# Memory cross-attention in a decoder trunk: the two heads of a group taken through one chain, with other delays behind the copies

## The chip, the core and the metric

One core of one Trainium2 chip runs the whole program. The metric is device microseconds from start to end of one execution, the median of several. Engines: PE (TensorE, matrix products), ACT (ScalarE), DVE (VectorE), POOL (GpSimd), SP (SyncE, which issues the transfers here). The times before are 1011.96, 1012.36 and 1012.1 us: median 1012.1 us.

## What is computed

A decoder trunk of two layers on 256 tokens of width 1024, all in fp32. Each layer is a SwiGLU feed-forward block at half weight, a mixing block, and a second feed-forward block. The mixing block of layer 0 has 4 mLSTM heads, that of layer 1 has 16 sliding-window heads (window 128, 2 key heads, partial rotary embedding, a learned sink per head). In both, 4 memory cross-attention heads of size 128 over 256 memory rows stand beside them, fed by the same input projection and the same output projection:

```python
proj = hn @ a_w_in[j]                     # layer 1: b_w_in[j]
y_tok = mlstm_heads(proj[..., :A_TOK], ...)   # layer 1: swa_heads(...)
y_mem = memory_heads(proj[..., A_TOK:], mem_k, mem_v, xa_q_norm_g[i], xa_k_norm_g[i])
x = x + jnp.concatenate([y_tok, y_mem], axis=-1) @ w_out

def memory_heads(xq, mem_k, mem_v, q_norm_g, k_norm_g):
    q = rms_norm(xq.reshape(bsz, t, M_HEADS, M_HD), q_norm_g)
    k = rms_norm(mem_k, k_norm_g)
    s = jnp.einsum('bthd,bmhd->bhtm', q, k) * M_HD ** -0.5
    p = jax.nn.softmax(s, axis=-1)
    return jnp.einsum('bhtm,bmhd->bthd', p, mem_v).reshape(bsz, t, M_Q)
```

## The kernel before

**Numbers and tiles.** Activations lie transposed, width on partitions, as tiles `[128, 2, 256]` (512 columns). For the projections every fp32 value is split into a high and a low part, and each tile product is three matmuls (`mm3`, lines 225, 226 and 227). A weight tile comes by a transfer into `wr` (5 buffers), ACT casts its high part into `wh` (line 211, 128x1024), DVE subtracts for the low part `wl` (line 212); 8 buffers each. Attention uses plain fp32 products: `mmf` (line 231; one instruction in the code is two or more passes on PE) and `transpose` (line 236). All results of PE go into one pool of 8 PSUM banks of `[128, 512]` fp32; `mo()` takes the next, and a bank comes free when its last reader is done.

**Who sets the order.** PE's and SP's order is that of the program text, and the text is interleaved by the class `Weave`. A main chain (projections, in pieces of 12 matmuls) runs; chains that were spawned beside it, each a Python generator, are stepped between its pieces once they are due. Due times are in a modelled clock, `wv.now`, which each product advances by a fixed cost; `yield d` means "not before d later", and the delays stand in one dictionary, `LAT` (lines 53 to 55). So `LAT` decides how many projection matmuls stand on PE between, say, a transposition and the product that reads its copy. ACT, DVE and POOL take their instructions in an order that a scheduler writes for each at build time; each engine then runs its own list strictly in order.

**Cross-attention, `cross_spawn`** (lines 568 to 611), for a group of two heads. `head_norm` (368 to 385) normalises the queries: a Square on ACT, a reduce on DVE (374), two small operations (377), a power on POOL (379), two small ones (381), and the multiplication (383), which is also the last reader of the group's projection bank. The chain `queries` transposes them (`turn`, 387) and copies them with a scale (`qT`, the ACT operation with `gqk`; all calls of the helper `act` show line 132). It spawns one chain `head(m)` for each of the two heads, `cross_s` later and `cross_m` between them. A head: two products into one bank (scores), a reduce for the maxima (591), two Exps on ACT with sums, a reciprocal (595), a multiplication (596); `cross_p` later four transpositions into one bank and a copy (603); `cross_o` later the values, two products into half of a bank, and `split_plain` of 256 columns (copy on ACT, line 245; subtraction on DVE, line 246). Then the head's rows of the output projection may be used (`ys.done`).

**Layer 1, `mixer_b`** (863 to 974). The main chain projects keys and values, the two cross query groups, and four query groups of four window heads each. Each query group goes through `head_norm`, rotary operations (857 to 860), `turn` and a scaled copy (`qr`, with `gcut`), and then two chains `head(ch)` (910 to 965), each for two window heads in two banks: a mask product into each bank (920), scores (925), reduces for maxima (929, 930), minima with the sinks (932, 933), four Exps and one for the sinks, sum and reciprocal (941, 942), four scalings (946); `head_p` later transpositions into two banks with two copies (954); `head_o` later values (961) and `split_plain`. Then the output projection: `out_proj` takes rows 8 to 11 (the cross heads) first, then 0 to 5, and last 6 and 7; `ys.has` steps other chains until a row's head is done. Layer 0, `mixer_a` (649 to 804), uses the same `cross_spawn` beside its mLSTM chains.

Of the kernel before, what the change touches and what calls it, by code (L numbers as in the profile page):

```python
# [10 lines left out]
F32 = mybir.dt.float32  # L11
# [3 lines left out]
AF = mybir.ActivationFunctionType  # L15
ALU = mybir.AluOpType
AX = mybir.AxisListType
PSUM = bass.MemoryType.PSUM

P = 128  # L20
T = 256
# [11 lines left out]
def constants():  # L33
# [16 lines left out]

LAT = dict(pieces=1, norm=7.5, norm_b=4.8, mnorm=2.4, x0=16.0, x0_b=7.5, mkeys=7.2, cross=9.5, cross_s=1.5,
           cross_m=3.7, cross_p=8.7, cross_o=3.0, gates=20.0, scores=2.2, scores_m=8.4, num=6.9, num_r=7.5,
           keys=5.5, keys_d=7.2, query=9.0, head=1.5, head_m=2.5, head_p=9.3, head_o=4.0)


WARM = 18
# [40 lines left out]
def tile_trunk(ctx: ExitStack, tc: tile.TileContext, a, out):  # L99
    nc = tc.nc  # L100
    seq = [0]

    def mk(pool, shape, dt, tag):
        seq[0] += 1
        return pool.tile(shape, dt, tag=tag, name=f"{tag}_{seq[0]}")
# [5 lines left out]
    wv = Weave()  # L111
# [16 lines left out]
    tt = nc.vector.tensor_tensor  # L128
    tabled = [None]

    def act(*args, **kw):
        ins = nc.scalar.activation(*args, **kw)  # L132
        if args[2] not in (AF.Copy, AF.Square):
            tabled[0] = ins
# [6 lines left out]
    def unit(dt):  # L141
        return mk(up, [P, 2, T], dt, "u")

    def tmp():
        return mk(tp, [P, 2, T], F32, "t")

    def col():
        return mk(cp, [P, 16], F32, "col")

    def mo():  # L150
        return mk(pb8, [P, 512], F32, "bank")

    def halves(ps):
        return ps.rearrange("p (h t) -> p h t", h=2)
# [48 lines left out]
    pieces = [1]  # L203
# [26 lines left out]
    def mmf(ps, lhsT, rhs, n, start=True, stop=True):  # L230
        nc.tensor.matmul(ps, lhsT, rhs, start=start, stop=stop, skip_group_check=True)  # L231
        wv.now += max(0.213, n * 0.00182)

    def transpose(ps, src):
        k = src.shape[0]
        nc.tensor.transpose(ps, src, ident[:k, :k])  # L236
        wv.now += 0.107
# [6 lines left out]
    def split_plain(src, hi, lo):  # L244
        nc.scalar.copy(hi, src)
        tt(out=lo, in0=src, in1=hi.bitcast(F32), op=ALU.subtract)
# [14 lines left out]
    class Norm:  # L261
# [30 lines left out]

        def chain(self, gap=LAT['norm_b']):
            pc = mo()
            for h in range(2):
                mmf(pc[:, h:h + 1], self.acc[:, 0, h * P:(h + 1) * P], ones, 1)
            self.rc = mk(sp, [P, 2], F32, "rc")
            rsqrt_cols(self.rc, pc[:, 0:2], 2, 1.0 / D)
            if not self.rows:
                self.done = True  # L300
                return
            yield gap
            ps = mo()
            bcast_rows(ps, self.rc)
            self.rb = mk(sp, [P, T], F32, "rb")
            nc.scalar.copy(self.rb, ps[:, :T])
            if self.half:
                self.hrb = mk(sp, [P, T], F32, "hrb")
                act(self.hrb, ps[:, :T], AF.Copy, scale=0.5)
            self.done = True  # L310
# [57 lines left out]
    def head_norm(dst, src, n, hsc):  # L368

        hd = src.shape[2] // n  # L370
        sq, v, u = tmp(), col(), col()
        sqv = sq[:, :, :n * hd]
        act(sqv, src, AF.Square)
        nc.vector.tensor_reduce(out=v[:, 0:2 * n].rearrange("p (h m) -> p h m", h=2),
                                in_=sqv.rearrange("p h (m d) -> p h m d", m=n), axis=AX.X, op=ALU.add)
        for h in range(2):
            nc.vector.tensor_scalar(u[:, n * h:n * h + n], v[:, n * h:n * h + n], hsc[:, h:h + 1], EPS,
                                    op0=ALU.mult, op1=ALU.add)
        nc.gpsimd.tensor_tensor(out=u[:, 8:8 + 2 * n], in0=u[:, 0:2 * n], in1=mhalf[:, 0:2 * n], op=ALU.pow)  # L379
        for h in range(2):  # L380
            nc.vector.tensor_scalar(v[:, 8 + n * h:8 + n * h + n], u[:, 8 + n * h:8 + n * h + n],
                                    hsc[:, 2 + h:3 + h], None, op0=ALU.mult)
        tt(out=dst.rearrange("p h (m d) -> p h m d", m=n), in0=src.rearrange("p h (m d) -> p h m d", m=n),  # L383
           in1=v[:, 8:8 + 2 * n].rearrange("p (h m) -> p h m", h=2).unsqueeze(3).to_broadcast([P, 2, n, hd]),
           op=ALU.mult)

    def turn(rows):

        ps = mo()
        for m in range(2):  # L390
            for h in range(2):
                transpose(ps[:, m * T + h * P:m * T + (h + 1) * P], rows[:, h, m * P:(m + 1) * P])
        return halves(ps)


    kT = [mk(cst, [P, 2, T], F32, f"kT{i}") for i in range(2)]
    vM = mk(cst, [P, 2, 512], F32, "vM")
    x0 = Norm(G_F1)

    def memory():  # L400
# [22 lines left out]
        def keys(gi, kr):  # L423
            nc.scalar.copy(kT[gi], turn(kr))
            return
            yield

        for gi in range(2):
# [13 lines left out]
            norm.fold()  # L442
            wv.spawn(norm.chain(), LAT['mnorm'])
            gv = Group(wkv, 512, mh, ml, rows=True)
# [5 lines left out]
            for i, q in enumerate((first, gr)):  # L450
                kr = tmp()
                head_norm(kr, q.ps, 2, hsc)
                wv.spawn(keys(i, kr), LAT['mkeys'] + 1.5 * i)
        for gi in range(2):
# [7 lines left out]
            if gi == 0:  # L462
                with tc.issue_after(last[0].ins):
                    for c2 in range(4):
                        x0.put(xT[c2])
                wv.spawn(x0.chain(LAT['x0_b']), LAT['x0'])

# [41 lines left out]
    def ffn(x, w_in, w_out, nxt=None, mid=None):  # L509
# [13 lines left out]
        for c2 in range(4):  # L523
# [25 lines left out]
            else:  # L549
                nxt.put(xn)  # L550
        wv.spawn(nxt.chain(), LAT['norm'])

# [15 lines left out]
    def cross_spawn(gr, gi, layer, hsc, ys):  # L568
        qn = unit(F32)
        head_norm(qn, gr.ps, 2, hsc)  # L570
        cell = []

        def queries():
            ps = turn(qn)
            qT = unit(F32)
            act(qT, ps, AF.Copy, scale=gqk[:, layer:layer + 1])
            cell.append(qT)
            for m in range(2):
                wv.spawn(head(m), LAT['cross_s'] + LAT['cross_m'] * m)
            return  # L580
            yield

        def head(m):
            hd, qT = gi * 2 + m, cell[0]
            hi, lo = ys.tiles(4 + gi)
            s = mo()
            for h in range(2):
                mmf(s[:, h * T:(h + 1) * T], qT[:, m, h * P:(h + 1) * P], kT[gi][:, m], T)
            sv = halves(s)
            c = col()  # L590
            nc.vector.tensor_reduce(out=c[:, 2:4], in_=sv, axis=AX.X, op=ALU.max, negate=True)  # L591
            p = unit(F32)
            for h in range(2):
                act(p[:, h], sv[:, h], AF.Exp, bias=c[:, 2 + h:3 + h], accum_out=c[:, 4 + h:5 + h])
            nc.vector.reciprocal(c[:, 6:8], c[:, 4:6])
            tt(out=p, in0=p, in1=c[:, 6:8].unsqueeze(2).to_broadcast([P, 2, T]), op=ALU.mult)
            yield LAT['cross_p']
            tps = mo()
            for mc in range(2):
                for h in range(2):  # L600
                    transpose(tps[:, mc * T + h * P:mc * T + (h + 1) * P], p[:, h, mc * P:(mc + 1) * P])
            pT = tmp()
            nc.scalar.copy(pT, halves(tps))
            yield LAT['cross_o']
            o = mo()
            for mc in range(2):
                mmf(o[:, :T], vM[:, mc, hd * P:(hd + 1) * P], pT[:, mc], T, mc == 0, mc == 1)
            split_plain(o[:, :T], hi[:, m], lo[:, m])
            ys.done.add(8 + hd)

        wv.spawn(queries(), LAT['cross'])


# [413 lines left out]
```

## Time and profile before

| | |
|---|---|
| runs | 1011.96, 1012.36, 1012.1 us |
| profiled execution | 1012.23 us, of which 1010.4 us is the span from its first to its last instruction |
| granted clock of PE | 1.00 of full speed |
| mixer_a | about 225 to 356 us of the span |
| mixer_b | about 718 to 845 us of the span |

How to read it: the profile shows one execution. A row of the timeline gives start, duration, engine, line, operation, output and inputs, and, in brackets, how long the engine was idle before it and what released it; "x4" are four instructions in a row of one shape. L12 is line 12 of the kernel. The view of waits adds up such idle times by what ended them, the view by windows gives busy times in a stretch, and the groups by line give busy us, mean ns of one and the idle time ahead. The rest of the span, outside the two mixers, is feed-forward work.

### The profile page before, as it was taken

To read this page: it belongs to the slowest core of one execution; us is meant where nothing else is said; L and a number is where in the kernel's file an instruction comes from. 1 tells how busy PE (TensorE), PEld (TensorE's weight loads), DVE (VectorE), ACT (ScalarE), POOL (GpSimd) and SP (SyncE) were. 2 spreads that over 40 slices of the span, in tenths; PEclk is the share of its full clock that TensorE was granted. 3 is DMA by queue.
4 is the path that set the end of the run, shared out by engine and by line. 5 is a ranking of instruction groups with operands and counts; after the bars stand their busy time and mean duration, and the time that the engine had idled before them with its cause. 6 is when DMAs were issued, how large, how long until landed. Compare 5 with 4: busy or idle time off the path is not lost.

```text
span 1010.4 us, 20624 instructions
## 1 busy us (share of the span) xinstructions
PE 998.5 (99%) x8594; PEld 980.2 (97%) x8594; DVE 655.5 (65%) x1063; ACT 519.5 (51%) x764; POOL 35.7 (4%) x32
## 2 busy tenths in 40 slices
PE   8999999999999999999999999999999999999998
PEld 7999999999999999999999999999987899999998
DVE  6866665577856676665558666656787766666551
ACT  7754445446656554444445544544557754454440
POOL 1200000000001000000000000000121000000000
PEclk9999999999999999999999999999999999999999
DMA  9776656666644566665676666567541347666550
GB/s 308 242 245 200 192 180 185 199 183 179 184 139 133 167 210 195 200 189 170 192 206 205 189 191 201 173 197 198 182 131 66 100 131 220 198 189 185 188 170 21
DMA packets 173204, 182.70 MB, mean 181 GB/s; under 512 B 7124, under 2 KB 168328, under 8 KB 173112
## 3 DMA queue, kind: packets, MB, share of 16 engines
q1 hardware_dynamic: 171872, 179.60, 58.3%
q10 hardware_dynamic: 1016, 1.58, 0.5%
q8 instruction: 67, 1.10, 0.5%
q0 software_dynamic: 224, 0.22, 0.2%
q14 instruction: 25, 0.20, 0.1%
HBM read 180.32 MB, written 1.05 MB: 180 GB/s over the span
## 4 chain that ended last, share of the span: by engine, by line
PE 94%; DVE 3%; ACT 1%; DMA 1%; POOL 0%; issue 0%; SPq 0%; ACTq 0%
PE bank L225 30%; PE bank L226 30%; PE bank L227 30%; PE bank L231 2%; PE bank L236 1%; ACT u L132 1%; DVE wl L212 1%; DMA wr<-in_mem_w_kv_dram 1%; PE bank L961 1%; POOL col L379 0%; DVE col L930 0%; DVE u L383 0%; DVE col L591 0%; PE bank L925 0%; DVE u L946 0%
## 5 line engine op out<-in xcount | busy, mean ns | idle before, releaser
L212 DVE TENSOR_TENSOR wl<-wr,wh 128x1024 fp32r<-128x1024 f32 (+1 forms) x347 | 414.7, 1196 | 279.8 <-ACT wh L211 279.0
L211 ACT CAST wh<-wr 128x1024 fp32r<-128x1024 f32 (+1 forms) x347 | 356.8, 1031 | 393.1 <-PE bank L226 368.9
L225 PE MATMUL bank<-xh,wh 128*128 128x256 f32 x1544 | 429.1, 278 | 0.0
L226 PE MATMUL bank<-xl,wh 128*128 128x256 f32 x1544 | 426.8, 276 | 0.0
L227 PE MATMUL bank<-xh,wl 128*128 128x256 f32 x1544 | 426.8, 276 | 0.0
L226 PEld LDWEIGHTS bank<-xl,wh 128*128 128x128 f32 x1544 | 290.3, 188 | 0.1
L225 PEld LDWEIGHTS bank<-xh,wh 128*128 128x128 f32 x1544 | 290.0, 188 | 0.1
L227 PEld LDWEIGHTS bank<-xh,wl 128*128 128x128 f32 x1544 | 289.9, 188 | 0.0
L225 PE MATMUL bank<-u,wh 128*128 128x256 f32 x896 | 249.3, 278 | 0.0
L226 PE MATMUL bank<-u,wh 128*128 128x256 f32 x896 | 247.6, 276 | 0.0
L227 PE MATMUL bank<-u,wl 128*128 128x256 f32 x896 | 247.6, 276 | 0.0
L225 PEld LDWEIGHTS bank<-u,wh 128*128 128x128 f32 x896 | 168.2, 188 | 1.9 <-issue 1.7
L226 PEld LDWEIGHTS bank<-u,wh 128*128 128x128 f32 x896 | 168.4, 188 | 0.1
L227 PEld LDWEIGHTS bank<-u,wl 128*128 128x128 f32 x896 | 168.3, 188 | 0.0
L225 PE MATMUL bank<-wh,xh 128*128 128x256 f32 x208 | 59.7, 287 | 0.0
L226 PE MATMUL bank<-wl,xh 128*128 128x256 f32 x208 | 57.9, 278 | 0.0
L227 PE MATMUL bank<-wh,xl 128*128 128x256 f32 x208 | 57.9, 278 | 0.0
L476 DVE TENSOR_TENSOR t<-bank,rb 128x256 f32<-128x256 f32 x88 | 36.6, 420 | 7.3 <-PE bank L227 7.3
L225 PEld LDWEIGHTS bank<-wh,xh 128*128 128x128 f32 x208 | 39.1, 188 | 0.5 <-issue 0.3
L226 PEld LDWEIGHTS bank<-wl,xh 128*128 128x128 f32 x208 | 39.1, 188 | 0.1
L227 PEld LDWEIGHTS bank<-wh,xl 128*128 128x128 f32 x208 | 39.0, 187 | 0.0
L479 DVE TENSOR_TENSOR t<-t,bank 128x256 f32<-128x256 f32 x88 | 32.7, 412 | 1.8 <-ACT t L132 1.8
(171 smaller groups left out, 657.5 us busy)
## 6 DMA issues: line engine op xcount, KB each, us to landing
wr<-in_ffn_w_in_dram SPq DMA_DIRECT2D x176, 512.0 KB, 3.6
wr<-in_ffn_w_out_dram SPq DMA_DIRECT2D x80, 512.0 KB, 3.5
wr<-in_a_w_in_dram SPq DMA_DIRECT2D x28, 512.0 KB, 3.9
wr<-in_b_w_in_dram SPq DMA_DIRECT2D x14, 512.0 KB, 4.6
wr<-in_a_w_out_dram SPq DMA_DIRECT2D x12, 512.0 KB, 3.3
wr<-in_b_w_out_dram SPq DMA_DIRECT2D x12, 512.0 KB, 3.4
wr<-in_ffn_w_out_dram SPq DMA_DIRECT2D x16, 256.0 KB, 2.8
wr<-in_mem_w_kv_dram SPq DMA_DIRECT2D x7, 512.0 KB, 8.0
```

What stands on the lines that cost most here:

```text
L132: ins = nc.scalar.activation(*args, **kw)
L211: last[0] = nc.scalar.copy(hi[:, i * n:(i + 1) * n], src[:, i * n:(i + 1) * n])
L212: tt(out=lo[:, i * n:(i + 1) * n], in0=src[:, i * n:(i + 1) * n], in1=hi[:, i * n:(i + 1) * n].bitcast(F32), op=ALU.subtract)
L225: nc.tensor.matmul(ps, wh, xh, start=start, stop=False, skip_group_check=True)
L226: nc.tensor.matmul(ps, wh, xl, start=False, stop=False, skip_group_check=True)
L227: nc.tensor.matmul(ps, wl, xh, start=False, stop=stop, skip_group_check=True)
L231: nc.tensor.matmul(ps, lhsT, rhs, start=start, stop=stop, skip_group_check=True)
L236: nc.tensor.transpose(ps, src, ident[:k, :k])
L476: tt(out=t[:, m], in0=ps[m][:, :T], in1=x.rb, op=ALU.mult)
L479: tt(out=t[:, m], in0=t[:, m], in1=ps[m][:, T:], op=ALU.mult)
L961: nc.tensor.matmul(o[es[e], cs], vr[:, i, js], pTs[e][:, src], start=i == 0, stop=i == 1, skip_group_check=True)
```

## The change

Both heads of a cross group now go through one chain, `heads()`: two score banks and four products in a row, the softmax of the one and the other, one pause `cross_p`, eight transpositions into two banks with two copies, one pause `cross_o`, then the values of both heads into the two halves of one bank (the first product of the first head alone has the start flag) and one `split_plain` of 512 columns in place of two of 256. Five delays are longer: `cross_s` 1.5 to 3.0, `cross_p` 8.7 to 11.0, `cross_o` 3.0 to 4.0, `head` 1.5 to 3.0 and `head_o` 4.0 to 4.5; `cross_m` (3.7) is gone. The three of the cross heads act in both mixers, `head` and `head_o` on the window heads of mixer_b. PE has as many instructions as before; ACT and DVE have four fewer each. The lines behind the change move by up to 9 (920 becomes 929, 925 934, 938 and 939 are the reduces, 946 becomes 955, 954 963, 961 970; in the cross heads 591 becomes 593, 603 608).

```diff
--- before.py
+++ after.py
@@ -50,9 +50,9 @@
 
 
 
-LAT = dict(pieces=1, norm=7.5, norm_b=4.8, mnorm=2.4, x0=16.0, x0_b=7.5, mkeys=7.2, cross=9.5, cross_s=1.5,
-           cross_m=3.7, cross_p=8.7, cross_o=3.0, gates=20.0, scores=2.2, scores_m=8.4, num=6.9, num_r=7.5,
-           keys=5.5, keys_d=7.2, query=9.0, head=1.5, head_m=2.5, head_p=9.3, head_o=4.0)
+LAT = dict(pieces=1, norm=7.5, norm_b=4.8, mnorm=2.4, x0=16.0, x0_b=7.5, mkeys=7.2, cross=9.5, cross_s=3.0,
+           cross_p=11.0, cross_o=4.0, gates=20.0, scores=2.2, scores_m=8.4, num=6.9, num_r=7.5,
+           keys=5.5, keys_d=7.2, query=9.0, head=3.0, head_m=2.5, head_p=9.3, head_o=4.5)
 
 
 WARM = 18
@@ -575,38 +575,47 @@
             qT = unit(F32)
             act(qT, ps, AF.Copy, scale=gqk[:, layer:layer + 1])
             cell.append(qT)
-            for m in range(2):
-                wv.spawn(head(m), LAT['cross_s'] + LAT['cross_m'] * m)
+            wv.spawn(heads(), LAT['cross_s'])
             return
             yield
 
-        def head(m):
-            hd, qT = gi * 2 + m, cell[0]
+        def heads():
+
+            qT = cell[0]
             hi, lo = ys.tiles(4 + gi)
-            s = mo()
-            for h in range(2):
-                mmf(s[:, h * T:(h + 1) * T], qT[:, m, h * P:(h + 1) * P], kT[gi][:, m], T)
-            sv = halves(s)
-            c = col()
-            nc.vector.tensor_reduce(out=c[:, 2:4], in_=sv, axis=AX.X, op=ALU.max, negate=True)
-            p = unit(F32)
-            for h in range(2):
-                act(p[:, h], sv[:, h], AF.Exp, bias=c[:, 2 + h:3 + h], accum_out=c[:, 4 + h:5 + h])
-            nc.vector.reciprocal(c[:, 6:8], c[:, 4:6])
-            tt(out=p, in0=p, in1=c[:, 6:8].unsqueeze(2).to_broadcast([P, 2, T]), op=ALU.mult)
+            ss, ps = [mo(), mo()], []
+            for m in range(2):
+                for h in range(2):
+                    mmf(ss[m][:, h * T:(h + 1) * T], qT[:, m, h * P:(h + 1) * P], kT[gi][:, m], T)
+            for m in range(2):
+                sv = halves(ss[m])
+                c = col()
+                nc.vector.tensor_reduce(out=c[:, 2:4], in_=sv, axis=AX.X, op=ALU.max, negate=True)
+                p = unit(F32)
+                for h in range(2):
+                    act(p[:, h], sv[:, h], AF.Exp, bias=c[:, 2 + h:3 + h], accum_out=c[:, 4 + h:5 + h])
+                nc.vector.reciprocal(c[:, 6:8], c[:, 4:6])
+                tt(out=p, in0=p, in1=c[:, 6:8].unsqueeze(2).to_broadcast([P, 2, T]), op=ALU.mult)
+                ps.append(p)
             yield LAT['cross_p']
-            tps = mo()
-            for mc in range(2):
-                for h in range(2):
-                    transpose(tps[:, mc * T + h * P:mc * T + (h + 1) * P], p[:, h, mc * P:(mc + 1) * P])
-            pT = tmp()
-            nc.scalar.copy(pT, halves(tps))
+            pTs = []
+            for m in range(2):
+                tps = mo()
+                for mc in range(2):
+                    for h in range(2):
+                        transpose(tps[:, mc * T + h * P:mc * T + (h + 1) * P], ps[m][:, h, mc * P:(mc + 1) * P])
+                pT = tmp()
+                nc.scalar.copy(pT, halves(tps))
+                pTs.append(pT)
             yield LAT['cross_o']
             o = mo()
-            for mc in range(2):
-                mmf(o[:, :T], vM[:, mc, hd * P:(hd + 1) * P], pT[:, mc], T, mc == 0, mc == 1)
-            split_plain(o[:, :T], hi[:, m], lo[:, m])
-            ys.done.add(8 + hd)
+            for m in range(2):
+                hd = gi * 2 + m
+                for mc in range(2):
+                    mmf(o[:, m * T:(m + 1) * T], vM[:, mc, hd * P:(hd + 1) * P], pTs[m][:, mc], T,
+                        m == 0 and mc == 0, mc == 1)
+            split_plain(halves(o), hi, lo)
+            ys.done.update((8 + 2 * gi, 9 + 2 * gi))
 
         wv.spawn(queries(), LAT['cross'])
```

## The prediction

> **What bounds the kernel now.** I read the page first: its busy line, then its shares of the chain that ended last.
>
> ```profile
> span 1010.4 us, 20624 instructions
> PE 998.5 (99%) x8594; PEld 980.2 (97%) x8594; DVE 655.5 (65%) x1063; ACT 519.5 (51%) x764; POOL 35.7 (4%) x32
> PE 94%; DVE 3%; ACT 1%; DMA 1%; POOL 0%; issue 0%; SPq 0%; ACTq 0%
> ```
>
> TensorE has work for 99% of the span. The change issues every matmul and transpose of before with the same shapes, so it can move the time only through the idle time of PE and through what PE loses between blocks of unlike instructions. The view by windows shows where that can be; the columns are length, PE, PE's loads, DVE, ACT, POOL, the granted clock, DMA share and GB/s.
>
> ```profile
> 255.00:290.00 35.00, 35.00 (x273) 33.75 (x272) 25.21 (x47) 21.32 (x44) 1.91 (x1) 1.00 0.48 146
> 740.00:760.00 20.00, 17.19 (x123) 14.33 (x121) 17.64 (x51) 13.70 (x44) 1.64 (x1) 1.00 0.31 100
> 760.00:780.00 20.00, 18.91 (x158) 16.50 (x158) 15.00 (x51) 14.43 (x43) 3.38 (x2) 1.00 0.19 62
> 780.00:800.00 20.00, 18.57 (x152) 14.81 (x152) 15.92 (x55) 12.17 (x41) 0.73 (x1) 1.00 0.33 99
> ```
>
> In mixer_a (255 to 290) PE is never idle. In mixer_b it lacks 5.3 us between 740 and 800, while DVE is busy for 88% of the first 20 us: there DVE and ACT nearly set the pace. The clock is 1.00 throughout and plays no part. What PE waited for there, 715 to 835 (total, times, longest):
>
> ```profile
> PE bank L231 <- ACT u L132: 1.5, 1, 1.5
> PE bank L925 <- ACT u L132: 1.4, 1, 1.4
> PE bank L231 <- ACT t L603: 1.1, 1, 1.1
> PE bank L920 <- DVE u L383: 0.7, 1, 0.7
> PE bank L961 <- ACT u L132: 0.4, 1, 0.4
> PE bank L920 <- ACT t L954: 0.2, 1, 0.2
> ```
>
> Six waits, 5.3 us. The next rows are PE's timeline (start, duration); I count from start to start, since a recorded end lies later than the next instruction can begin.
>
> ```profile
> 734.50 0.28 PE L225 MATMUL bank<-wh,xh 128*128 128x256 f32 x1
> ...
> 735.80 0.28 PE L227 MATMUL bank<-wh,xl 128*128 128x256 f32 x1
> 735.91 1.03 PE L231 MATMUL bank<-kT,u 128*128 128x256 f32 x4
> 736.59 0.47 PE L225 MATMUL bank<-wh,xh 128*128 128x256 f32 x1
> ```
>
> The matmul of 735.80 is shown as ending at 735.80 + 0.28 = 736.08, yet the next starts at 735.91, so 0.17 us of an end is pipeline. A wait thus costs its row plus some 0.16 us, and the six 5.3 + 6 x 0.16 = **6.3 us**. More than that, and the small losses between blocks, can't be won.
>
> **The change part by part.**
>
> *Slots of PE.* Four passes of L231 take 0.68 us to the next start and make that one 0.47 instead of 0.28 long: 0.87 in all.
>
> ```profile
> 751.08 1.13 PE L231 MATMUL bank<-t,vM 128*128 128x256 f32 x4 [1.05 <-ACT t L603]
> 752.05 0.49 PE L920 MATMUL bank<-maskb,identb 128*128 128x384 bf16 x2
> 752.47 0.93 PE L925 MATMUL bank<-u,u 64*128 64x128 f32 x8
> 753.32 0.66 PE L236 MATMUL bank<-con,u 128*128 128x128 f32 x4
> 753.81 0.49 PE L920 MATMUL bank<-maskb,identb 128*128 128x384 bf16 x2
> ```
>
> So after a stall four passes take 0.97, a mask pair 0.42, eight score passes 0.85, four transposes 0.49 (0.44 elsewhere, and less ahead of a projection block); twelve projection matmuls take 1.41 (734.50 to 735.91), 0.1175 each.
>
> *Waits that go.* The first L231 row (1.5: scores of cross group 1 wait for the scaled queries), the third (1.1: values wait for the copy of the transposes) and, by the moved order, the 0.7, 0.4 and 0.2 are not met again in their places. In the order in which the changed program issues its instructions, cross values stand a mask pair, twelve or more projection matmuls or eight score passes behind the second copy, so the 1.1 goes. The others come back in another form.
>
> *Wait A, scores of cross group 1.* Now the four Exps of both heads of group 0 stand on ACT ahead of the scaled copy that these scores read.
>
> ```profile
> 737.26 2.54 POOL L379 TENSOR_TENSOR col<-col,mhalf 128x8 f32<-128x8 f32 x1 [3.40 <-DVE col L377]
> 739.84 0.36 DVE L381 TENSOR_SCALAR col<-col,qsc 128x4 f32<-128x4 f32 x2 [1.53 <-POOL col L379]
> 740.11 0.68 DVE L591 TENSOR_REDUCE col<-bank 128x2 f32<-128x512 f32 x1
> 740.71 0.68 DVE L383 TENSOR_TENSOR u<-bank,col 128x512 f32<-128x512 f32 x1
> 740.82 0.47 ACT L132 ACTIVATE u<-bank,col 128x256 f32<-128x256 f32 x1 [4.59 <-DVE col L591]
> 741.74 0.69 ACT L132 ACTIVATE u<-bank,gqk 128x512 f32<-128x512 f32 x1
> 742.30 1.05 ACT L211 CAST wh<-wr 128x1024 fp32r<-128x1024 f32 x1
> ```
>
> DVE issues L381 at 739.84 (POOL's power holds it, as before), L383 from 740.30, the first reduce from 740.91, three rotary operations, the second reduce from 741.99 (0.60 a 512-wide one, start to start). Two Exps with their accumulators take 0.92 (740.82 to 741.74): 741.62 to 742.54, 742.70 to 743.62; the copy ends 0.69 later, at 744.31. PE had the first scores at 735.91; now twelve more matmuls stand ahead of them (1.41), and from them to group 1's scores come 8 passes 1.72, transposes 0.36 and 36 matmuls 4.32: 743.72. To 744.35, 0.04 behind the copy, **A is 0.64** with rounding, where 1.6 stood.
>
> *Wait B, scores of the first window head (L934 after, L925 before).* They read the scaled copy of query group 0, which now stands behind four Exps of cross group 1; their reduces stand behind the L381 of the next query group, which waits for POOL. Behind the Exps of 742.54 DVE has a reciprocal, an L212 (1.13 to the next start), two multiplies and the group's reduce (0.60 each) and small ones with their hand-overs, so that this power starts at about 746.5, beside the next L212, and takes the 2.54 of 737.26: 749.08. Then L381 749.12, reduce 749.39, L383 749.99, reduce 750.60; Exps to 751.02 and to 752.23, copy to 752.92. PE, from 744.35 on, has 8 score passes 1.82, four transposes 0.36, 24 matmuls 2.86, eight transposes 0.88 and the mask pair 0.42: 6.34, there at 750.69. **B is 2.27**, where 1.6 stood. Twelve matmuls of query group 2 and all later heads are queued behind it on PE, in order, so it counts in full.
>
> *Wait E, a bank.* Two score banks at once and two transposed banks at once turn the eight banks over faster. By the changed order the fourth transposed tile of the first two window heads goes into the bank that held query group 2, which L383 of that group has to read first, and that L383 now stands on DVE behind the softmax of two window heads. From 752.96 I walk DVE and ACT:
>
> ```profile
> 753.84 1.22 DVE L212 TENSOR_TENSOR wl<-wr,wh 128x1024 fp32r<-128x1024 f32 x1
> 755.31 0.28 DVE L929 TENSOR_REDUCE col<-bank 128x1 f32<-128x128 f32 x1
> 756.48 0.16 DVE L932 TENSOR_TENSOR col<-col,nsink 128x4 f32<-128x4 f32 x1
> 756.68 0.37 ACT L132 ACTIVATE u<-bank,col 128x128 f32<-128x128 f32 x1 [2.02 <-DVE col L932]
> 758.27 0.21 ACT L132 ACTIVATE col<-col 128x4 f32<-128x4 f32 x1
> 758.93 1.01 DVE L946 TENSOR_SCALAR u<-u,col 128x128 f32<-128x128 f32 x4
> 749.44 1.64 POOL L379 TENSOR_TENSOR col<-col,mhalf 128x8 f32<-128x8 f32 x1 [9.64 <-DVE col L377]
> ```
>
> A head's reduces to its L932 take 1.17 (755.31 to 756.48), its Exps 1.6 to 1.7 (756.68 to 758.27 and one more), the four scalings 0.92. L212 ends at 755.03; reduces; Exps of head 0 to 758.1; a copy (0.56, 741.74 to 742.30) and an L211 to 759.6; beside them scalings, the reduces of head 1 and an L212 (1.13) to 761.66; Exps of head 1 761.86 to 763.45; split of the cross values, ACT to 764.12 and DVE to 764.76; scalings to 765.68; L374 0.61 and small ones to 766.9; POOL's power 1.64 or 2.54; L381, L383: **769.82 or 770.72**. PE has from 752.96: 0.85 + 1.52 (twelve matmuls) + 0.46 + 1.27 (a head's mask and scores) + 1.82 (values of two cross heads) + 0.90 + 1.27 + 1.52 + 1.35 + 1.82 + 0.99 (three groups of transposes) = 13.77, so is there at 766.73. **E is 3.1 or 4.0.** Before, the like wait was the 0.7 of the list.
>
> The power took 1.64 at 749.44 and 2.54 at 737.26, where an L212 began 0.17 before it. Here four scalings begin beside it. No row shows those beside a power, so I keep both ends and take the middle.
>
> ```profile
> L946 DVE TENSOR_SCALAR u<-u,col 128x256 f32<-128x256 f32 x16 | 5.6, 348 | 0.0
> L946 DVE TENSOR_SCALAR u<-u,col 128x128 f32<-128x128 f32 x16 | 4.5, 282 | 0.1
> ```
>
> In the groups by line, 128 columns more cost a scaling 66 ns (348 - 282). [...]
>
> *Small waits.* A bank of the second window head waits for Exps: 0 to 0.4, taken 0.1. One waits for L246 of cross values: 0.2. Four groups of window transposes on two banks wait for their copies: 0.75, before 0.7 with its pipeline share. Sum after: 0.64 + 2.27 + 0.1 + (3.1 to 4.0) + 0.2 + 0.75 = **7.1 to 8.0**, against 6.3.
>
> *Fewer blocks.* The paired scores and values leave about six breaks fewer between unlike blocks, 0.1 us each (0.97 against 0.87), while one split of 512 in place of two of 256 spares DVE and ACT time that the walks above already have. In mixer_b two values of window heads now run back to back at two places.
>
> ```profile
> 771.46 1.45 PE bank L961 x16
> 777.79 0.80 PE bank L961 x8
> ```
>
> Sixteen passes 1.45 against twice 0.80 is 0.15. In all 0.7 to 1.0 saved, taken 0.75; ends 0 and 1.3.
>
> *mixer_a.* It has no wait now and DVE 25.21 of 35 us; I expect none after. Its ends: nothing, and one 512-wide reduce (0.68, row above) that comes ahead of a copy that scores read. I take 0. *Weights.* No load is moved on the queue past another; the banks and weight buffers come free in the same order, and in these windows the transfers use 19 to 33% of the DMA engines. I take 0; a late tile would cost at most its cast and its subtraction (1.05 and 1.22, rows above).
>
> **Sum.** 7.1 to 8.0 - 6.3 - 0.75 = +0.05 to +0.95, middle **+0.4** on the profiled execution: 1010.4 of span and 1.83 around it, 1012.23, to 1012.6. The median of the runs shown, 1012.1, is 0.1 below that; I predict 1012.5.
>
> **The rivals.**
>
> *Slower: the hand-overs between DVE and ACT.* From 753 to 770 the chain of E changes engine some 17 times. I gave 0.03 to 0.05 to each, as at 740.79 to 740.82 (the reduce's end, the Exp's start). If the scheduler's order makes DVE or ACT finish something else first at several of them, the walk grows, and every us of it stands in E at full price, because E's cover (13.77) is used up already. At 0.1 each E is 1.7 larger, and B, with six, 0.5: 1012.5 + 2.1 = **1014.6**. It decides once the chain is 1.6 longer than I walk it. For it: DVE's 88% in 740 to 760. Against: the rows of hand-overs seen.
>
> *Faster: E is hidden.* If L383 of query group 2 runs before the softmax of the second window head (its square and reduce need only a bank that PE finished at 755), the bank is free when PE comes: -3.55, **1009.0**. For it: before, the same wait cost 0.7 only. Against: DVE takes its instructions in the built order, and there L374 stands behind the scalings.
>
> *Nothing changes hands.* The waits only swap names and come to the same sum: 1012.1. For it: PE's 99%.
>
> **How the numbers follow.** Forecast (1011.9 to 1013.2) 0.55, slower rival 0.25, faster rival 0.15, nothing 0.05. About 0.2%, 2.0 us, is what a measurement of this kernel can tell from no change: bounds 1010.1 and 1014.1. Faster has its rival's 0.15 and 0.02 of the forecast's tail (mixer_a and blocks at their good ends); slower the 0.25 less what falls below 1014.1, with the forecast's upper tail, 0.26; the rest is 0.57. The range 1009.6 to 1014.9 leaves out about half of the faster rival and under half of the slower.
>
> **What would show it.** In the changed profile: the span near 1010.8; PE's waits in mixer_b on L231 for an ACT u of about 0.5, on L934 for an ACT u of about 2.1, and on L236 for DVE's L383 of 3 to 4 near 767; none on L231 for the copy of L608; no wait of PE in mixer_a. The power before that L383 of 1.6 or 2.5 us says which end of E holds. I'm wrong if E's wait is absent or above 5, if a DMA ends a wait of PE, or if mixer_a's PE is idle at all.

## The result, and the profile after

The changed kernel takes 1020.2 us (median of 1020.01, 1020.11, 1020.26 and 1021.34) against 1012.13 before: a ratio of 1.0082, 95% interval 1.0064 to 1.0099. It is slower by 8 us, outside the predicted range. The profiled execution took 1020.11 us, 7.9 more than the one shown of before. The page's first lines of the changed kernel:

```profile
span 1018.3 us, 20617 instructions
PE 1006.7 (99%) x8594; PEld 988.5 (97%) x8594; DVE 655.0 (64%) x1059; ACT 519.2 (51%) x760; POOL 33.7 (3%) x32
```

PE has the same 8594 instructions and is busy for 8.2 us longer (998.5 before). So the loss is not idle time. PE's waits between 700 and 840, the answer to the six of before:

```profile
PE bank L934 <- ACT u L132: 1.9, 1, 1.9
PE bank L236 <- DVE u L383: 1.8, 1, 1.8
PE bank L231 <- ACT u L132: 0.4, 1, 0.4
PE bank L929 <- DVE u L246: 0.3, 1, 0.3
PE bank L236 <- ACT t L963: 0.3, 1, 0.3
PE bank L929 <- ACT t L963: 0.2, 1, 0.2
```

These are the waits that the prediction named, B, E, A and the small ones. They add up to 4.9 us, less than the 5.3 of before, and mixer_a has none.

Where did the time go, then? I compare the start of PE's n-th matmul in the two traces, as both have the same number. The changed kernel is 0.02 us early to the end of the first feed-forward block, 0.22 late behind mixer_a, **0.94** late at the 6900th (815.11 against 814.17, near the end of the attention of mixer_b; 0.80 six matmuls on, where both are past it), 1.56 at the 7100th (838.49), and then loses steadily: 4.41 at the 7800th, 6.18 at the 8200th, 7.9 at the end. Of the 8 us, 7 are lost behind the attention, where the change touches nothing.

The view by windows of that last block, first before, then after (the count behind PE's busy time is of the matmuls that touch the stretch, some two more than start in it; the 1.00 is the granted clock):

```profile
870.00:910.00 40.00, 40.00 (x355) 40.00 (x354) 25.68 (x36) 19.98 (x23) 0.00 (x0) 1.00 0.63 190
950.00:1000.00 50.00, 50.00 (x443) 50.00 (x443) 23.06 (x25) 15.43 (x17) 0.00 (x0) 1.00 0.43 132
```

```profile
870.00:910.00 40.00, 40.00 (x342) 40.00 (x341) 24.64 (x33) 18.60 (x22) 0.00 (x0) 1.00 0.58 185
950.00:1000.00 50.00, 50.00 (x427) 50.00 (x426) 25.71 (x29) 18.06 (x20) 0.00 (x0) 1.00 0.44 138
```

PE is never idle and at full clock in both, and gets through 13 matmuls fewer in 40 us. Its timeline shows how: before, nine matmuls from start to start,

```profile
899.73 0.28 PE L226 MATMUL bank<-xl,wh 128*128 128x256 f32 x1
...
900.75 0.28 PE L226 MATMUL bank<-xl,wh 128*128 128x256 f32 x1
```

and after, eight:

```profile
899.83 0.28 PE L225 MATMUL bank<-xh,wh 128*128 128x256 f32 x1
...
900.77 0.28 PE L227 MATMUL bank<-xh,wl 128*128 128x256 f32 x1
```

1.02 / 9 = 0.1133 us before, 0.94 / 8 = 0.1175 after; over the whole block the means are 0.1133 and 0.1178. The two numbers stand in one trace, too: before, PE ran at 0.1133 through nearly all of the feed-forward blocks from 55 to 718, at 0.1178 through most of mixer_b, and from 813.94 at 0.1133 again, but for 47 matmuls about 837. I call them the fast and the slow pace. In both traces the projection matmuls of a row have one or the other (but for twelve of the changed kernel from 754.44, at half clock, with 0.213), and a pace changes at or a few matmuls behind a place where something else stands between (transpositions, attention, the small products of a norm); within an unbroken row it changed at two places in each trace, near 34 and near 252 us.

After the change, 167 matmuls from 816 to 835 (the last four rows of the output projection and the first 72 matmuls of the last block) and the 1463 of the last block from 842 on are slow: 1630 x 4.45 ns = 7.2 us, less 47 in between that are fast where before they were slow (0.2): **7.0**. With the 0.94 that is the 7.9.

### The profile page after: what moved, and what is told of

Same layout as the page of the kernel before. It is cut to its first block, busy times and chain, and to the rows that moved or that the text cites. A ratio compares the mean times of both kernels' runs of the same rounds, so it can differ in the third digit from the quotient of the medians.

```text
span 1018.3 us, 20617 instructions
## 1 busy us (share of the span) xinstructions
PE 1006.7 (99%) x8594; PEld 988.5 (97%) x8594; DVE 655.0 (64%) x1059; ACT 519.2 (51%) x760; POOL 33.7 (3%) x32
## 4 chain that ended last, share of the span: by engine, by line
PE 93%; DVE 3%; POOL 1%; ACT 1%; DMA 1%; issue 0%; SPq 0%; ACTq 0%; DVEq 0%; POOLq 0%
PE bank L225 30%; PE bank L226 30%; PE bank L227 29%; PE bank L231 2%; POOL col L379 1%; PE bank L236 1%; DVE wl L212 1%; DMA wr<-in_mem_w_kv_dram 1%; PE bank L934 0%; PE bank L970 0%; DVE col L374 0%; DVE u L383 0%; ACT u L132 0%; ACT t L963 0%; DVE col L377 0%
## 5 line engine op out<-in xcount | busy, mean ns | idle before, releaser
L212 DVE TENSOR_TENSOR wl<-wr,wh 128x1024 fp32r<-128x1024 f32 (+1 forms) x347 | 414.5, 1196 | 286.3 <-ACT wh L211 285.4
```

Source lines behind the costliest of these rows:

```text
L212: tt(out=lo[:, i * n:(i + 1) * n], in0=src[:, i * n:(i + 1) * n], in1=hi[:, i * n:(i + 1) * n].bitcast(F32), op=ALU.subtract)
```

## The experiments

Theory P (pace): the 7 us are the slow pace of the last stretches, which a restart of the stream happens to fall into; the attention matters only in that it moves when and behind what the stream restarts. Theory M (mixer): the changed attention leaves something behind that slows the rest. Theory G, a form of it: the granted clock, which fell to a half after wait B. The windows of the changed kernel show that fall:

```profile
754.00:755.00 1.00, 1.00 (x6) 0.56 (x3) 0.93 (x1) 1.00 (x3) 0.00 (x0) 0.50 0.02 8
755.00:756.00 1.00, 1.00 (x7) 1.00 (x6) 1.00 (x5) 0.01 (x1) 0.00 (x0) 0.50 0.00 0
756.00:757.00 1.00, 1.00 (x7) 1.00 (x7) 0.67 (x4) 0.36 (x3) 0.00 (x0) 0.54 0.74 242
```

Medians stand beside those of before in the same comparison; executions of before scatter by some 1.6 us with their granted clock (1011.56 to 1012.46 at a mean of 0.999 or 1.000, or 1013.43 to 1014.35 at 0.997 or 0.998, but for two named further down; in the traces of e4 and e6 the first 50 us stood at 0.97, in that of before at 1.00).

### An extra break in the last block (e1 to e5, e9, e10, e13, e14, e16)

All of these leave the attention alone and put small products into a bank that nobody reads, ahead of one group of the last feed-forward block:

```diff
         for gi in range(11):
+            if gi in extra:                      # e1, e3: (2,)   e2: (2, 7)
+                pd = mo()
+                for h in range(2):
+                    mmf(pd[:, h:h + 1], ident, ones, 1)
             ps = [mo(), mo()]
```

> The changed kernel, with two extra one-column products into a bank that nobody reads, put between groups 1 and 2 of the last feed-forward block (behind mixer_b and both norm steps). Theory P (pace): in an unbroken run of projection matmuls PE starts one every 0.1133 or one every 0.1178 us; it keeps the pace until something else stands between, and each of the two one-column or broadcast steps of a norm turned it over in both traces. Then the 1392 matmuls behind the extra break run at 0.1133: 1392 x 4.4 ns = 6.2 us less, 0.3 for the break: 1014.3 us. Theory M (the mixer left something behind, such as the clock that was granted at half near 754, or a buffer order, that slows the rest): nothing in the feed-forward block undoes it, 1020.5 us.

Measured 1021.44 (before 1012.43). The break didn't turn the pace: slow ahead of it and behind it (342 matmuls from 870 to 910, as in the changed kernel). My reading that any step of this kind turns the pace over fell for these two products; the norm's own steps do turn it, as e16 below shows.

> The changed kernel with the extra break of e1 ahead of group 2 and once more ahead of group 7 of the last feed-forward block. Theory P: fast pace between the two breaks only, 480 matmuls x 4.4 ns = 2.1 us less and two breaks of 0.3: 1018.7 us. If an extra break helps by itself, not by turning the pace over, it is at least as fast as e1. Theory M: 1020.8 us.

Measured 1022.32: slow throughout, as e1 (profiled executions 1021.32 and 1020.62).

> The kernel before with the extra break of e1 ahead of group 2 of the last feed-forward block. Theory P: its fast pace is turned into the slow one for 1392 matmuls: 1012.1 + 6.2 + 0.3 = 1018.6 us, without any of the change. Theory M: 1012.4 us.

Measured 1012.85 (ratio 1.0003, 0.9994 to 1.0012). Fast ahead and behind. None of the three tells P from M; they tell that a break isn't enough.

Four transpositions in the place of the two products, ahead of group 2 (e4 changed, e5 before), or ahead of group 8 (e9):

```diff
-                for h in range(2):
-                    mmf(pd[:, h:h + 1], ident, ones, 1)
+                for h in range(4):
+                    transpose(pd[:, h * P:(h + 1) * P], ident)
```

> The changed kernel with four transpositions of the identity, in place of the one-column products, ahead of group 2 of the last feed-forward block. Breaks by four transpositions left the pace as it was in both traces (before 729, 733 and 789; after 729 and 790). Theory P with that reading: slow pace stays, 1020.7 us. If any break draws the pace anew, it may also be 1014.5. Theory M: 1020.7 us.

Measured 1016.3 (1013.87 to 1018.46, eight executions, each below every one of the changed kernel). The windows of e4, and its timeline at the break (the transpositions and the next matmul):

```profile
870.00:910.00 40.00, 40.00 (x355) 40.00 (x355) 25.47 (x33) 18.65 (x22) 0.00 (x0) 1.00 0.62 195
950.00:1000.00 50.00, 50.00 (x444) 50.00 (x443) 26.09 (x29) 18.73 (x20) 0.00 (x0) 1.00 0.46 143
```

```profile
854.42 0.60 PE L236 MATMUL bank<-con 128*128 128x128 f32 x4
854.77 0.37 PE L225 MATMUL bank<-xh,wh 128*128 128x256 f32 x1
```

355 and 444 again: the stream came in slow (72 matmuls from 846, the last nine in 1.06 us, 853.36 to 854.42) and went out fast. Four transpositions that compute nothing gave back about half of the loss. The wide scatter has another place: the profiled execution, 1018.46, was 1.8 us late ahead of mixer_b and 5.0 at the 6900th matmul. There the clock had stayed up at wait B (1.00 from 740 to 770) and fell behind wait E:

```profile
770.00:775.00 5.00, 3.28 (x16) 3.28 (x17) 3.01 (x13) 2.05 (x9) 0.48 (x1) 0.58 0.00 0
```

That is 3.2 us in mixer_b, where the changed kernel's own profile lost 0.72.

> The kernel before with the four extra transpositions of e4 ahead of group 2 of the last feed-forward block. In e4 they turned the slow pace into the fast one; in e1 to e3 one-column products left either pace as it was. Theory P with a break that swaps: slow for 1392 matmuls, 1012.4 + 6.2 + 0.3 = 1018.9 us, with the attention of before untouched. Theory P with a break that always restarts at the fast pace: 1012.7 us. Theory M (what the mixer left is what e4 mended): 1012.7 us, and no matmul of the last block at 0.1178.

Measured 1012.66 (ratio 0.9993, 0.998 to 1.0006): fast to fast.

> The changed kernel with the four extra transpositions of e4 ahead of group 8 instead of group 2 of the last feed-forward block. Theory P: if they turn the pace here too, 576 matmuls more stay slow than in e4, 2.6 us: about 2.6 us above e4 and 3.5 us below the changed kernel, 1017 us; if not, the slow pace stays to the end, 1020.5 us. A theory by which the transpositions mend something other than the pace has no reason for the 2.6.

Measured 1017.89, 1.6 above e4 and 2.3 below the changed kernel, the scatter of e4 allowing no more than the order. The trace says it plainly, slow ahead of group 8 and fast behind it:

```profile
870.00:910.00 40.00, 40.00 (x342) 40.00 (x341) 23.94 (x32) 18.10 (x21) 0.00 (x0) 1.00 0.59 185
950.00:1000.00 50.00, 50.00 (x444) 50.00 (x443) 25.58 (x30) 18.72 (x20) 0.00 (x0) 1.00 0.47 151
```

Ten restarts in one execution (e10), one to ten transpositions:

```diff
-                for h in range(4):
-                    transpose(pd[:, h * P:(h + 1) * P], ident)
+                for h in range(gi):              # extra=tuple(range(1, 11))
+                    transpose(pd[:, h % 4 * P:(h % 4 + 1) * P], ident)
```

> The changed kernel with one transposition of the identity ahead of group 1 of the last feed-forward block, two ahead of group 2, and so on to ten ahead of group 10: ten restarts of the stream in one execution. Theory P with the pace drawn at each restart: stretches of 0.1133 and of 0.1178 us both, each unbroken until the next restart (or settled within its first few matmuls), and no other pace. If transpositions always restart at the fast pace: all ten at 0.1133 and about 1014.5 us with 55 transpositions (some 6 us) on top, 1020 us.

Measured 1021.59, one execution. Behind one transposition the stream was slow for 24 matmuls, up to the next small products of the norm, and fast behind those. Behind two to seven it was fast after one to four slow matmuls, behind eight and nine slow, behind ten fast after four slow ones (65 matmuls in 7 us from 900, behind six; 91 in 10.5 from 920.5, behind eight; 88 in 10 from 933, behind nine; 478 in 54 from 946, behind ten). Only the two paces occur.

So eight or nine should bring the slow pace into the kernel **before** (e13, e14): the same edit in it, `range(8)` or `range(9)` ahead of group 2.

> The kernel before, its attention untouched, with eight transpositions of the identity ahead of group 2 of the last feed-forward block. In e10 the stream came out of eight and of nine of them at 0.1178. Theory P: if it does here, 1392 matmuls x 4.4 ns = 6.2 us and some 1.0 us for the transpositions: about 1019.5 us; if it comes out fast, 1013.2. Theory M: 1013.2 us, as nothing ahead of the block is changed.

Measured 1019.26 against 1012.33, ratio 1.0076 (1.0062 to 1.009).

> As e13 with nine transpositions. Theory P: 1019.6 us when the stream comes out slow, 1013.3 us when fast; one of the two at least is met with each pace seen in the last block, and nothing between that the first 50 us or the clock don't explain. Theory M: 1013.3 us.

Measured 1019.2, ratio 1.007 (1.0057 to 1.0082). The windows of e13, and its timeline at the break:

```profile
870.00:910.00 40.00, 40.00 (x342) 40.00 (x341) 24.66 (x34) 18.83 (x23) 0.00 (x0) 1.00 0.60 186
950.00:1000.00 50.00, 50.00 (x427) 50.00 (x426) 25.65 (x29) 17.63 (x19) 0.00 (x0) 1.00 0.41 133
```

```profile
848.58 1.04 PE L236 MATMUL bank<-con 128*128 128x128 f32 x8
849.38 0.36 PE L225 MATMUL bank<-xh,wh 128*128 128x256 f32 x1
```

This decides it. Up to the break e13 runs as before (0.03 us early at the 6900th matmul). Eight transpositions, 0.8 us of work, cost 7 us, and the counts are those of the changed kernel: 342 and 427. The slow pace needs nothing of the change.

The other way round, the changed kernel with one transposition ahead of group 1 (e16):

```diff
-                for h in range(4):
-                    transpose(pd[:, h * P:(h + 1) * P], ident)
+                transpose(pd[:, :P], ident)      # extra=(1,)
```

> The changed kernel with a single transposition of the identity ahead of group 1 of the last feed-forward block; in e10 the stream was fast from there to the next break. Theory P: if it comes out fast, only the attention and its waits are left of the difference to before, +1 us by the trace of the changed kernel at the end of the attention, +0.75 for the slow last rows of the output projection and 0.2 for the transposition: 1013.5 to 1014.5 us. If it comes out slow: 1020.5 us. Theory M: 1020.4 us.

Measured **1014.0** against 1012.19: ratio 1.0019 (1.001 to 1.0029). Its windows and waits:

```profile
870.00:910.00 40.00, 40.00 (x355) 40.00 (x354) 25.95 (x35) 19.53 (x23) 0.00 (x0) 1.00 0.61 197
950.00:1000.00 50.00, 50.00 (x443) 50.00 (x442) 23.61 (x26) 16.09 (x18) 0.00 (x0) 1.00 0.42 133
```

```profile
PE bank L937 <- ACT u L132: 1.9, 1, 1.9
PE bank L236 <- DVE u L383: 1.8, 1, 1.8
```

The attention is that of the changed kernel, waits and all (its lines stand 3 lower); the last block is at 355 and 443. One transposition of 0.1 us gave back 6.2 of 8. Of the 1.8 that stay, 0.7 are the 167 matmuls from 816 on, still slow (167 x 4.45 ns), 0.1 the transposition, and about 1 us the attention of both mixers.

But the transposition didn't turn slow into fast by itself, as its timeline shows:

```profile
837.72 0.28 PE L227 MATMUL bank<-xh,wl 128*128 128x256 f32 x1
...
838.74 0.28 PE L227 MATMUL bank<-xh,wl 128*128 128x256 f32 x1
838.86 0.27 PE L236 MATMUL bank<-con 128*128 128x128 f32 x1
839.20 0.28 PE L227 MATMUL bank<-xh,wl 128*128 128x256 f32 x1
...
841.68 0.28 PE L227 MATMUL bank<-xh,wl 128*128 128x256 f32 x1
841.79 0.61 PE L231 MATMUL bank<-con,rc 128*128 128x128 f32 x4
842.48 0.28 PE L227 MATMUL bank<-xh,wl 128*128 128x256 f32 x1
...
843.50 0.28 PE L227 MATMUL bank<-xh,wl 128*128 128x256 f32 x1
```

Ahead of it nine matmuls take 1.02 us, the fast pace. Behind it 21 take 2.48, the slow pace, as behind the single one of e10. Then come the four products of a norm (L231), and behind them nine take 1.02 again. It is the norm that turned the stream to fast, because the transposition had made it slow ahead of the norm.

The norms do so nearly everywhere. A norm interrupts the stream twice, each time with four passes of L231: first those on `acc`, then those on `rc`. In the 18 traces here (mean of the last gaps ahead, and of those from the fifth to the fourteenth behind) the second step turned the pace over in 90 of 90 places and the first in 108 of 126; 17 of the 18 exceptions are the first norm of the program, near 25 us, and the other is in e7. Two such steps stand between the output projection and the bulk of the last block, so the block mostly gets the pace in which the stream leaves the attention. That was slow in all ten traces with the changed attention and its delays, and fast in the six with the attention of before. To that extent theory M is right: what the change leaves behind is the pace, and nothing more is needed, as e13 shows.

### A break ahead of the last rows (e15)

```diff
         wts = [wrow(kc) for kc in late]
+        if nxt.gi == G_F2 + 8:
+            pd = mo()
+            for h in range(4):
+                transpose(pd[:, h * P:(h + 1) * P], ident)
```

> The changed kernel with four transpositions of the identity ahead of the last two rows of mixer_b's output projection, behind all attention. Theory P: whatever pace comes out, the time is the mixer's part (+1 us against before at that place) and 0.4 for the transpositions, with 4.4 ns for each matmul behind that is slow: 1013.5 to 1014 us with the last block fast, 1020 with it slow. Theory M: 1020.5 us.

Measured 1020.65, slow to slow (851 matmuls from 900 to 1000); the pace missed. But in its profiled execution the clock didn't fall in the mixer (1.00 from 740 to 760, with wait B in it, and from 770 to 780, behind wait E), so it shows the waits alone:

```profile
PE bank L236 <- DVE u L383: 3.0, 1, 3.0
PE bank L938 <- ACT u L132: 1.9, 1, 1.9
```

### The wait and the clock (e6)

The two mask products of the first window head six times each, in the place of wait B:

```diff
             for s in sc:
-                nc.tensor.matmul(s[:, :384], identb, maskb[:, :384], start=True, ...)
+                for _ in range(6 if ch == 0 else 1):
+                    nc.tensor.matmul(s[:, :384], identb, maskb[:, :384], start=True, ...)
```

> The changed kernel, with each of the first window head's two mask products issued six times (the later ones overwrite, the result is the same), some 2.1 us of work in place of the wait on L934 for the scaled copy. Theory G (the granted clock of 0.50 near 754, after that wait, costs the time, there or later): the clock stays at 1.00 and most of the 8 us go, 1013 to 1015 us. Theory P: the clock may stay, and PE then reaches the transpositions that wait for L383 some 1.5 us earlier and waits there longer; the time follows the pace of the last block alone: 1020 us at 0.1178, 1013.5 if this edit happens to turn it.

Measured 1021.45 (1019.73 to 1027.18). B was filled (1.9 to 0.5) and the clock stayed at 1.00 there (750 to 760); but PE waited longer for L383 (3.0), the clock fell behind that wait (0.76 from 770 to 775), and the last block was slow (342 and 427). The profiled execution, 1023.92, had 2 us of its loss in the first 50 us, where the clock was 0.97.

```profile
PE bank L236 <- DVE u L383: 3.0, 1, 3.0
PE bank L935 <- ACT u L132: 0.5, 1, 0.5
```

Theory G falls for the 7 us: without the half clock at 754 they are still there, in the last block (e6, e15). For the attention the traces say where the half clock costs. Behind wait B it is nearly free (0.72 us lost in mixer_b with it, 0.48 in e15 without), since PE is held until DVE's L383 anyway and only waits less there (1.8 for 3.0). Behind wait E less hides it: 2.0 lost in e9, with 3.4 us at half clock, and 3.2 in e4, with 6.8.

### The two halves of the change (e7, e8)

e7 is the changed kernel with the dictionary of delays of before; e8 is the kernel before with the five new delays, `cross_m` staying at 3.7.

> One chain for both heads, with the delays of before. Theory P: up to the last block it may differ by some us through its own waits; the last block then runs wholly at 0.1133 or wholly at 0.1178 (6.5 us apart), whatever the waits were. Theory M: the chains make a part of the 8 us of their own, waits that can be pointed to in mixer_b; e7 and e8 together make the 8.

Measured 1018.66, ratio 1.0047 (1.0031 to 1.0063).

> The chains of before, one for each head (3.7 apart), with the other delays of the change. Theory P: as e7, the last block at one pace, the difference to before up to the output projection no more than its waits of PE. Theory M: the delays make the part of the 8 us that e7 doesn't show.

Measured 1015.65, ratio 1.0022 (1.0004 to 1.0039). In both profiles the last block is fast (355 and 443 in e7, 355 and 444 in e8), and what they lose lies in mixer_b: 5.2 us by the 6900th matmul in e7, 3.4 in e8, where the whole change loses 0.9. The largest waits of e7, and the largest of e8:

```profile
PE bank L225 <- DVE u L383: 2.5, 1, 2.5
PE bank L231 <- ACT u L132: 1.9, 1, 1.9
PE bank L236 <- ACT u L132: 1.5, 2, 1.2
```

```profile
PE bank L236 <- DVE u L383: 4.4, 1, 4.4
```

Paired heads without the delays find their copies late, and the delays without the pairing make the bank wait E larger. In both profiles the clock then stood at 0.50 for 6.8 us (780.2 to 787.0 in e7, 784.5 to 791.3 in e8), and part of these losses is that; how much, no run here separates. In these executions the two halves belong together: each alone is worse in the attention than both, though each alone comes out faster than the whole, because its last block is fast.

### Another order of the three products (e11, e12)

```diff
-        nc.tensor.matmul(ps, wh, xl, start=False, stop=False, skip_group_check=True)
-        nc.tensor.matmul(ps, wl, xh, start=False, stop=stop, skip_group_check=True)
+        nc.tensor.matmul(ps, wl, xh, start=False, stop=False, skip_group_check=True)
+        nc.tensor.matmul(ps, wh, xl, start=False, stop=stop, skip_group_check=True)
```

> The changed kernel with the three products of every split tile in the order high x high, low weight x high, high weight x low, so that the weights loaded in a row are high, low, high. Theory W (the slow pace comes from the load of the low weights or of the same high weights twice in a row beside a running matmul): one pace only, 0.1133 throughout would be 1012 us and less, 0.1178 throughout 1020 to 1050 us. Theory P without a part for the order: both paces are still met, and the last block has one of them.

Measured 1020.2, but not one time: seven executions from 1018.93 to 1022.16, one of 1012.99 and one of 1015.15. The profiled one (1020.34) is slow in the last block (427 from 950 to 1000). One program thus gave times 7 us apart; that the low ones had the fast pace is argued from the size, as they have no trace.

> The kernel before with the product order of e11. Theory W: the same single pace as in e11, so that the difference of e12 to e11 is that of the mixers alone, under 1.5 us. Theory P without a part for the order: the last block has one of the two paces, whichever the restart gives: 1012.5 or 1019 us.

Measured 1011.61 (ratio 0.9994, 0.9985 to 1.0004), fast in the last block (443). Theory W falls: both paces are met with this order as well. No version here is shown to be faster than the kernel before.

## Why the prediction was wrong

**The step that failed** is the second sentence on what bounds the kernel: the change "can move the time only through the idle time of PE and through what PE loses between blocks of unlike instructions". It took the length of a projection matmul for fixed. The rows to doubt it were in the trace of before: I read 0.1175 from 734.50 to 735.91 and never read a feed-forward block, where the same instruction took 0.1133. With the slow pace in the last stretches as a rival, 1630 matmuls x 4.4 ns = 7.2 us, it would have stood at 1019.7, beside 1020.2 measured. No step of mine could have told which pace the restart gives, so its chance would have been a guess.

**Point by point, for the rest.** Wait A: 0.64 forecast, 0.44 and 0.16 of pipeline measured. Wait B: 2.27, against 1.9 and 0.16. The walk to wait E went by these rows of the changed kernel:

```profile
746.74 2.54 POOL L379 TENSOR_TENSOR col<-col,mhalf 128x8 f32<-128x8 f32 x1 [6.72 <-DVE col L377]
767.47 1.64 POOL L379 TENSOR_TENSOR col<-col,mhalf 128x8 f32<-128x8 f32 x1 [18.18 <-DVE col L377]
```

```profile
746.58 1.22 DVE L212 TENSOR_TENSOR wl<-wr,wh 128x1024 fp32r<-128x1024 f32 x1
767.25 1.03 DVE L955 TENSOR_SCALAR u<-u,col 128x128 f32<-128x128 f32 x4
769.61 0.68 DVE L383 TENSOR_TENSOR u<-bank,col 128x512 f32<-128x512 f32 x1
```

The first power began at 746.74, forecast about 746.5, and took 2.54 beside its L212, as forecast. The second took 1.64 beside four scalings (767.25 to 768.28): the low end of E was right. L383 ended at 770.29, forecast 769.82, and 0.22 of the difference came from mixer_a. In both kernels a power of 128x8 took 2.48 to 2.54 where an L212 stood beside it (737.26 and 771.96 before, 737.48 and 746.74 after) and 1.64 alone (779.09 before, 780.42 after). Beside the scalings it was no longer than alone, here and in nine more of the traces; no run shows 2.54 beside them, so the 0.9 us between the two ends of E didn't come. E itself was 1.8 instead of 3.1 because PE, at half clock from 754 to 757, came later; in e15, with full clock, it is 3.0, and 3.2 with its pipeline share.

mixer_a has no wait, as forecast, yet lost 0.22: some 25 more of its matmuls ran at the slow pace, which is half of it. No transfer ended a wait of PE in the mixer: right. **The sum** of the mechanisms was forecast at +0.05 to +0.95 and is 0.80 to 0.94 at the end of the attention in the profiled execution, and about 1 us in e16: at its upper end, right in kind, a little over the +0.4 that I took. It had no term for a fall of the clock behind wait E, which made the loss in mixer_b 3.2 in the profiled execution of e4. The slower rival (longer hand-overs between DVE and ACT) ends near the right side for the wrong reason: the hand-overs were as short as read, and the chain was not longer. The faster rival didn't come: E is there.

What stays open is why a break gives one pace or the other, and so why the changed attention leaves the stream slow. Four transpositions turned the slow pace in e4 and e9 and kept it in e15; two one-column products (e1) kept it at the place where those of e4 turned it; attention values led to both (before, 0.1133 from 778.52 and 0.1178 from 800.71). In most kernels here the pace came out alike in every execution, to judge by the times; in e11 it didn't, and of 27 executions of before in the comparison with e5 to e8 two took 1019.24 and 1020.59 against 1011.98 to 1014.35 for the rest, which looks like it without a trace to prove it; so does one of twelve executions of e8, 1021.95 against 1014.87 to 1017.17.

## What to carry to other kernels

When a kernel keeps one engine busy from end to end, compare the start-to-start time of its commonest instruction stage by stage, before and after: here equal work ran at two paces, 0.1133 and 0.1178 us a matmul, and 7 of the 8 us were that. Before blaming or crediting an edit, align the two traces by instruction number and look where the distance grows; if it grows in a stage that the edit doesn't touch, put a dummy instruction there in **both** kernels and see whether the difference moves with it. And judge such an edit at equal pace: here 1.0082 became 1.0019 with one transposition.

## What the runs showed of the hardware that I had not expected

The split matmuls of 256 columns, each with its own weight load, ran back to back at 0.1133 or at 0.1178 us, with nothing between and at a granted clock of 1.00 in both cases: two spacings for one shape, at one clock. The unbroken row of 1464 in the last block kept its pace to the end, 0.1133 before (840.35 to 1006.26) and 0.1178 after (841.80 to 1014.19). Small products of another kind between them turned the pace over at most of the norms: the second step did in 90 of 90 places, the first in 108 of 126.

The clock fell to 0.50 for 3.4 us behind a wait of 1.9 us in four traces (the changed kernel, e1, e2, e16) and not behind the same 1.9 in four others (e4, e9, e10, e15), nor behind the 1.5 and 1.4 of before. Behind a wait of 3.0 it fell in e4 (for 6.8 us), e6, e9 and e10, and not in e15. At 0.50 nine of the same matmuls took 1.92 us from start to start (the changed kernel, 754.82 to 756.74), 0.213 each in place of 0.1178. So the same wait was followed by the half clock in one execution and not in another; what decides it no run here shows.
